# A two-layer diffusion block on one core: GpSimd's weight split and decay masks move to VectorE and TensorE, and column spreads move to ScalarE four at a time

## The chip, the cores and the metric

One core of a Trainium2 chip runs the whole program in one launch. The metric is the device time in microseconds; the kernel before was timed three times. A profile of one further execution gives the rows below. Engines in them: PE is TensorE (PEld its weight loads), DVE is VectorE, ACT is ScalarE, POOL is GpSimd, SP is SyncE, which here issues most DMAs.

## The reference, cut to what matters

Two layers follow each other over 256 latent and 256 context tokens of width 1024. Layer 0 mixes with latent attention plus retention, layer 1 (the second mixer) with a gated delta net; after each mixer comes a layer of 16384 experts (`peer`), which is most of the arithmetic. The change lies mostly in the second mixer:

```python
qkv = jax.nn.silu(short_conv(jnp.concatenate([q, k, v], -1), conv_w))   # z = h @ w_in
q = l2_norm(q) * DN_DK ** -0.5 ; k = l2_norm(k)
decay = jnp.where(incl, jnp.exp(jnp.where(incl, gdiff, 0.0)), 0.0)
lmat = jnp.where(strict, einsum(kb, kc) * decay, 0.0)
t_inv = triangular_solve(eye + lmat, eye)
attn = einsum(qc, kc) * decay
y = rms_norm(o, norm_g) * silu(gate)          # gated_out
```

## The kernel before, in words

All of it is one program of Python loops; the framework's scheduler orders each engine's queue, and each queue then runs strictly in that order, an instruction waiting at its head for what it needs. Full precision is had from three fp32r products: `split` (L262) makes a high part (ACT copies to fp32r, L268) and a low part (a subtraction, L271), and `mm3` (L256) multiplies high by high, high by low and low by high.

The second mixer is `deltanet`. Its stages in the trace:

- 1729 to 2057 us, projections and inverses. `heads` takes 32 weight chunks of 128x1024 (`weights`, L1234: DMA `dw`, ACT `dwsh`, GpSimd `dwsl`, two buffers each), multiplies (`dz`), convolves over five taps (ACT the first, DVE four: L1320, L1322, tile `cv`), and normalises q and k: squares, column sums, `rstd_steps` on DVE (tiles `r4..`, `r2..`, `dr`), then `row_bcast` per 128 tokens. At the same time `inv_rows` builds the triangular matrices `BT` from `decay` (tile `E`) and key products, `inv_solve` (L1415, L1416) solves their 32-blocks on DVE one step after another, and `inv_join` joins the blocks.
- 2057 to 2146 us, the recurrence over chunks (`recur`), with `queries`, which calls `decay` again for q (`Eq`).
- 2146 to 2196 us, `gated`: the root-mean-square of each head's output, its spread (`orb`), the gate, the output product `yo`.

`row_bcast` (L357) turns a column of 128 values into a row that stands in all partitions: DVE multiplies a tile of ones by the column (tile `gcol`, 128x128, three buffers), and PE multiplies it by the identity. Four calls fill one 512-wide PSUM tile. It is called 16 times in `gated`, 48 times in `heads`, 8 times in `low` (first mixer) and 48 times in `gate_row`. `decay` (L1363) makes on PE the sums of the log decays, exponentiates on ACT, and GpSimd multiplies by a 0/1 mask (L1372), 16 times for the inverses and 8 times for the queries.

Of the kernel before, what the change touches and what calls it, by code (L numbers as in the profile page):

```python
# [10 lines left out]
F32 = mybir.dt.float32  # L11
F32R = mybir.dt.float32r
# [4 lines left out]
ALU = mybir.AluOpType  # L17
# [4 lines left out]
P = 128  # L22
D = 1024
KD = D // P
# [218 lines left out]
class Model:  # L243
# [102 lines left out]
    def gate_row(self, pool, ps, l, m, s):  # L346
        nc = self.nc
        t = pool.tile([P, D], F32, name=f"gate{l}{m}{s}")
        for h in range(2):
            o = ps.tile([P, 512], F32, tag="ps", name=f"adag{l}{m}{s}{h}")  # L350
            for k in range(4):
                self.row_bcast(pool, o[:, k * P:(k + 1) * P], self.mod[l, m][:, h * 4 + k, s:s + 1])
            nc.scalar.copy(t[:, h * 512:(h + 1) * 512], o)
        return t


    def row_bcast(self, pool, out, col):  # L357
        self.n += 1
        g = pool.tile([P, P], F32, tag="gcol", name=f"gcol{self.n}", bufs=3)
        self.nc.vector.tensor_scalar_mul(g, self.c["ones"], col)  # L360
        self.mm(out, g, self.c["ident"])

    def rstd(self, out, x, scale, eps):

# [98 lines left out]
    def mixer0(self, open_x, open_h):  # L463
        nc, a, c = self.nc, self.a, self.c
# [15 lines left out]
        rg = pq.tile([P, 4, T2], F32, name="rg")  # L480
# [17 lines left out]
        with ExitStack() as e2:  # L498
            p = self.pool(e2, "m0ada", 1, side="right")
# [13 lines left out]
        p1 = self.pool(ep, "m0t", 1, side="right")  # L513
# [15 lines left out]
        def low():  # L529
            sqs = []  # L530
            for j in range(3):
                nc.scalar.copy(cq[:, j, :], zs[j])
                sq = p1.tile([P, T2], F32, tag="sq", name=f"sq{j}", bufs=3)
                nc.scalar.activation(sq, cq[:, j, :], AF.Square)
                sqs.append(sq)
            yield

            ss = ps.tile([P, 8], F32, tag="ps", name="cqss")
            for tb in range(4):
                sl = slice(tb * P, (tb + 1) * P)  # L540
                self.mm(ss[:, tb:tb + 1], sqs[0][:, sl], c["ones"][:, :1], True, False)
                self.mm(ss[:, tb:tb + 1], sqs[1][:, sl], c["ones"][:, :1], False, True)
                self.mm(ss[:, 4 + tb:5 + tb], sqs[2][:, sl], c["ones"][:, :1])
            v = p1.tile([P, 8], F32, name="cqv")
            nc.vector.tensor_scalar(v[:, :4], ss[:, :4], 1.0 / 256, 1e-6, ALU.mult, ALU.add)
            nc.vector.tensor_scalar(v[:, 4:], ss[:, 4:], 1.0 / 128, 1e-6, ALU.mult, ALU.add)
            r = p1.tile([P, 8], F32, name="cqr")
            nc.scalar.activation(r, v, AF.Sqrt)
            nc.vector.reciprocal(r, r)
            nc.vector.tensor_mul(v, v, r)  # L550
            nc.vector.tensor_mul(v, v, r)
            nc.vector.tensor_scalar(v, v, -0.5, 1.5, ALU.mult, ALU.add)
            nc.vector.tensor_mul(r, r, v)
            yield
            for b in range(2):
                o = ps.tile([P, T2], F32, tag="ps", name=f"cqb{b}")
                for tb in range(4):
                    self.row_bcast(p1, o[:, tb * P:(tb + 1) * P], r[:, b * 4 + tb:b * 4 + tb + 1])
                for i in ((0, 1), (2,))[b]:
                    g = qn[:, i:i + 1] if i < 2 else kvn  # L560
                    nc.vector.scalar_tensor_tensor(cq[:, i, :], cq[:, i, :], g, o, ALU.mult, ALU.mult)
                    nc.scalar.copy(cs[0][:, i, :], cq[:, i, :])
                    nc.vector.tensor_sub(cs[1][:, i, :], cq[:, i, :], cs[0][:, i, :].bitcast(F32))
            yield
            w = pw.tile([P, 512], F32, tag="w", name="uv", bufs=2)
            nc.sync.dma_start(w, a["uv"])
            ws = self.split(pw, w, [P, 512], "arw")
            yield
            for tb in range(4):
                o = ps.tile([P, 512], F32, tag="ps", name=f"vm{tb}")  # L570
                sl = slice(tb * P, (tb + 1) * P)
                self.mm3(o, (cs[0][:, 2, sl], cs[1][:, 2, sl]), ws, True, True)
                nc.scalar.copy(VM[:, tb, :], o)
# [62 lines left out]
        p = self.pool(ea, "m0at", 3)  # L636
# [133 lines left out]
        with ExitStack() as e2:  # L770
            p = self.pool(e2, "m0o", 1, side="right")
            w = []
            for k in range(KD):
                r = p.tile([P, D], F32, tag="woutr", name=f"woutr{k}", bufs=3)
# [5 lines left out]
            x = open_x()  # L780
            p = self.pool(e2, "m0n", 1, side="right")
# [14 lines left out]
            h = open_h()  # L796
# [416 lines left out]
    def deltanet(self, hs, next_h, open_x, ahead, xt):  # L1213
        nc, a, c = self.nc, self.a, self.c
# [10 lines left out]
        p = self.pool(es, "dn", 1, side=side)  # L1225
# [8 lines left out]
        def weights(src, nm):  # L1234
            w = pw.tile([P, KD, P], F32, tag="w", name="dw" + nm, bufs=2)
            nc.sync.dma_start(w, src)
            return self.split(pws, w, [P, KD, P], "dws", bufs=2, eng=nc.gpsimd)


        def gates(pw, pv):  # L1240
# [45 lines left out]
            nc.vector.tensor_scalar_mul(sm["negc"], sm["negc"], -1.0)  # L1286

        cw, known = c["dn_conv"], set()

        def heads(kind, h0, pool, bufs, ps):
# [58 lines left out]
            for i in range(2):  # L1351
                h = h0 + i
                o = ps.tile([P, 512], F32, tag="ps", name=f"qb{n}{i}")
                for tb in range(nb):
                    self.row_bcast(pv, o[:, tb * P:(tb + 1) * P], r[:, i, tb:tb + 1])
                if kind == 0:
                    nc.vector.scalar_tensor_tensor(qT[:, h, :], cv[:, i, :], P ** -0.5, o[:, :T], ALU.mult, ALU.mult)
                else:
                    nc.vector.tensor_mul(kT[:, h, :], cv[:, i, :], o)
                    known.add(h)  # L1360


        def decay(pool, tg, h0, d, n, tag, bufs):  # L1363
            mr, ml = (("le", "gt"), ("ge", "lt"))[d]
            u = slice(d * 8 + h0, d * 8 + h0 + 4)
            rg = pool.tile([P, 4, P], F32, tag="rg", name="rg" + n, bufs=2)
            nc.vector.tensor_tensor(rg, c[mr].unsqueeze(1).broadcast_to([P, 4, P]), sm["g"][:, tg, u].unsqueeze(2).broadcast_to([P, 4, P]), ALU.mult)
            o = ps.tile([P, 512], F32, tag="ps", name="gd" + n)
            self.mm(o, c[ml], rg.rearrange("p u i -> p (u i)"))
            E = pool.tile([P, 4, P], F32, tag=tag, name="E" + n, bufs=bufs)  # L1370
            nc.scalar.activation(E, o.rearrange("p (u i) -> p u i", u=4), AF.Exp)
            nc.gpsimd.tensor_mul(E, E, c[mr].unsqueeze(1).broadcast_to([P, 4, P]))  # L1372
            return E, rg


# [242 lines left out]
        def gated(h):  # L1618
            ov = oT[:, h:h + 2, :]
            sq = po.tile([P, 4, P], F32, tag="sq", name=f"osq{h}")  # L1620
            nc.scalar.activation(sq, ov.rearrange("p h (b t) -> p (h b) t", t=P), AF.Square)
            o = ps.tile([P, 4], F32, tag="ps", name=f"oss{h}")
            for i in range(4):
                self.mm(o[:, i:i + 1], sq[:, i, :], c["ones"][:, :1])
            r = po.tile([P, 4], F32, tag="r", name=f"or{h}")
            self.rstd(r, o, 1.0 / P, "e6")
            yield
            o = ps.tile([P, 512], F32, tag="ps", name=f"orb{h}")
            for i in range(4):
                self.row_bcast(po, o[:, i * P:(i + 1) * P], r[:, i:i + 1])  # L1630
            nc.vector.scalar_tensor_tensor(ov, ov, ng, o.rearrange("p (h t) -> p h t", h=2), ALU.mult, ALU.mult)
            nc.vector.scalar_tensor_tensor(ov, ov, 0.5, gT[:, h:h + 2, :], ALU.mult, ALU.mult)
            nc.scalar.copy(yh[:, h:h + 2, :], ov)
            nc.vector.tensor_sub(yl[:, h:h + 2, :], ov, yh[:, h:h + 2, :].bitcast(F32))
            yield
            for k in (h, h + 1):
                w = po.tile([P, D], F32, tag="w", name=f"wo{k}", bufs=2)
                nc.sync.dma_start(w, a["dn_out"][:, k, :])
                ws = self.split(po, w, [P, D], "wo", bufs=3)
                for tb in range(NTB):  # L1640
                    for hf in range(2):
                        if k == 0:
                            ys.append(ps.tile([P, 512], F32, tag="ps", name=f"yo{tb}{hf}"))
                        sl, hl = slice(tb * P, (tb + 1) * P), slice(hf * 512, (hf + 1) * 512)
                        self.mm3(ys[tb * 2 + hf], (yh[:, k, sl], yl[:, k, sl]), (ws[0][:, hl], ws[1][:, hl]), k == 0, k == KD - 1)
# [150 lines left out]
```

## Time and profile before

| | us |
|---|---|
| runs | 3101.31, 3096.46, 3106.05 (median 3101.31) |
| the profiled execution's own time | 3091.57 |
| its span, first to last instruction | 3089.8 |
| PE busy | 2792.0 (90%) |
| DVE busy | 2307.7 (75%) |
| ACT busy | 1272.9 (41%) |
| POOL busy | 747.8 (24%) |

Busy shares are over the whole span, most of which is the two expert stages; the change acts in 467 us of it, from 1729 to 2196 us, so the stage's own rows have to be read.

### The profile page before, as it was taken

What the parts mean: (1) busy time and instruction counts of PE and PEld (TensorE: products, weight loads), DVE (VectorE), ACT (ScalarE), POOL (GpSimd) and SP (SyncE); (2) the same over time, 40 slices, a digit from 0 to 9 for tenths busy, and PEclk for the clock granted to TensorE, in tenths of its full rate; (3) what the DMA queues carried; (4) which work ended last, traced back from release to release, by engine and by line L of the source; (5) the groups of instructions that cost most, each with busy time, mean ns of one, the idle gap of its engine ahead of it and who ended that gap; (6) DMA issues with size and microseconds to landing.
All of it is one profiled execution on the core that took longest, in us unless ns stands there. A gap on an engine that the chain in (4) does not pass through costs nothing.

```text
span 3089.8 us, 44817 instructions
## 1 busy us (share of the span) xinstructions
PE 2792.0 (90%) x16843; PEld 2424.3 (78%) x16843; DVE 2307.7 (75%) x4500; ACT 1272.9 (41%) x2141; POOL 747.8 (24%) x469
## 2 busy tenths in 40 slices
PE   8989999988999799999999778668888899999997
PEld 4766788877789688888899566657887789999996
DVE  2966599996999899999544687877799665555555
ACT  3235333683333233333333335322348454444443
POOL 2310234001045756665000234414320100000000
PEclk9989999999999899999999889779899999999999
DMA  6531323669999799999542112322347876666663
GB/s 232 183 117 35 109 83 133 231 253 332 323 374 400 289 399 377 395 399 375 180 150 94 68 54 82 91 56 76 129 147 263 284 241 216 207 213 209 213 211 109
DMA packets 272170, 643.87 MB, mean 208 GB/s; under 512 B 36464, under 2 KB 138992, under 8 KB 267472
## 3 DMA queue, kind: packets, MB, share of 16 engines
q1 hardware_dynamic: 225120, 487.50, 47.0%
q0 software_dynamic: 38768, 142.49, 11.9%
q10 hardware_dynamic: 8064, 11.01, 1.0%
q8 instruction: 132, 2.16, 0.3%
q14 instruction: 86, 0.70, 0.1%
HBM read 583.77 MB, written 57.15 MB: 207 GB/s over the span
## 4 chain that ended last, share of the span: by engine, by line
PE 38%; DVE 16%; DMA 11%; issue 6%; POOL 4%; ACT 3%; POOLq 0%; SPq 0%; ACTq 0%; DVEq 0%
PE f L254 16%; PE act L254 15%; DMA vr<-p_v 3%; DMA rowv<-p_v,rowe 3%; DMA ur<-p_u 2%; DVE cv L1322 2%; PE dz L254 2%; POOL rowv L1061 1%; POOL rowu L1061 1%; DVE vsl L271 1%; DVE usl L271 1%; DVE rowy L1078 1%; DVE adaj L341 1%; DVE rowu L1068 1%; DMA adat<-ada_t 1%
## 5 line engine op out<-in xcount | busy, mean ns | idle before, releaser
L254 PE MATMUL f<-vsl,gsh 128*128 128x512 f32 x1260 | 498.3, 397 | 28.6 <-DVE vsl L271 28.5
L254 PE MATMUL f<-vsh,gsh 128*128 128x512 f32 x1260 | 489.6, 397 | 21.7 <-ACT gsh L268 14.1
L254 PE MATMUL f<-vsh,gsl 128*128 128x512 f32 x1260 | 495.4, 395 | 4.6 <-DVE gsl L271 4.6
L271 DVE TENSOR_TENSOR vsl<-vr,vsh 128x1024 fp32r<-128x1024 f32 x252 | 303.9, 1238 | 192.4 <-ACT vsh L268 191.5
L271 DVE TENSOR_TENSOR usl<-ur,ush 128x1024 fp32r<-128x1024 f32 x240 | 295.0, 1229 | 165.3 <-ACT ush L268 161.5
L268 ACT ACTIVATE ush<-ur 128x1024 fp32r<-128x1024 f32 x256 | 270.0, 1055 | 261.5 <-PE act L254 168.2
L254 PE MATMUL act<-hp0h,usl 128*128 128x384 f32 x1024 | 346.7, 339 | 15.7 <-DVE usl L271 12.9
L254 PE MATMUL act<-hp0h,ush 128*128 128x384 f32 x1024 | 347.9, 340 | 5.2 <-ACT ush L268 4.3
L254 PE MATMUL act<-hp0l,ush 128*128 128x384 f32 x1024 | 345.2, 337 | 0.0
L268 ACT ACTIVATE vsh<-vr 128x1024 fp32r<-128x1024 f32 x252 | 257.2, 1052 | 213.0 <-PE f L254 139.7
L268 ACT ACTIVATE gsh<-gelu 128x384 fp32r<-128x384 f32 (+1 forms) x256 | 119.9, 470 | 498.5 <-DVE gelu L1168 395.8
L254 PEld LDWEIGHTS f<-vsl,gsh 128*128 128x128 f32 x1260 | 240.1, 191 | 84.2 <-DVE vsl L271 38.0
L254 PEld LDWEIGHTS f<-vsh,gsh 128*128 128x128 f32 x1260 | 238.6, 191 | 78.3 <-ACT vsh L268 17.3
L254 PE MATMUL act<-hp1h,usl 128*128 128x256 f32 x1024 | 294.2, 287 | 4.6 <-DVE usl L271 4.6
L254 PE MATMUL act<-hp1h,ush 128*128 128x256 f32 x1024 | 295.0, 288 | 1.2 <-ACT ush L268 1.2
L254 PE MATMUL act<-hp1l,ush 128*128 128x256 f32 x1024 | 294.6, 288 | 0.0
L254 PEld LDWEIGHTS f<-vsh,gsl 128*128 128x128 f32 x1260 | 239.7, 190 | 55.7 <-DVE gsl L271 6.0
L1061 POOL DMA_INDIRECT rowu<-p_ur,rowe x128 | 175.2, 1369 | 279.0 <-DVE rowa L1068 182.7
L1061 POOL DMA_INDIRECT rowv<-p_v,rowe x128 | 186.9, 1460 | 95.5 <-DVE rowy L1078 72.0
L254 PEld LDWEIGHTS act<-hp0h,usl 128*128 128x128 f32 x1024 | 193.8, 189 | 18.7 <-DVE usl L271 14.5
L254 PEld LDWEIGHTS act<-hp1h,usl 128*128 128x128 f32 x1024 | 200.3, 196 | 5.9 <-DVE usl L271 5.6
L254 PEld LDWEIGHTS act<-hp1h,ush 128*128 128x128 f32 x1024 | 200.3, 196 | 3.6 <-ACT ush L268 1.4
(773 smaller groups left out, 5961.1 us busy)
## 6 DMA issues: line engine op xcount, KB each, us to landing
ur<-p_u SPq DMA_DIRECT2D x256, 512.0 KB, 4.5
vr<-p_v SPq DMA_DIRECT2D x256, 512.0 KB, 4.5
adat<-ada_t SPq DMA_DIRECT2D x80, 512.0 KB, 5.8
W<-wst SPq DMA_DIRECT2D x20, 2048.0 KB, 7.3
w<-W SPq DMA_DIRECT2D x32, 768.0 KB, 9.6
wq<-p_wq SPq DMA_DIRECT2D x32, 512.0 KB, 3.4
dw<-dn_in SPq DMA_DIRECT2D x32, 512.0 KB, 3.3
w<-W SPq DMA_DIRECT2D x32, 512.0 KB, 5.6
```

The source lines that it names most:

```text
L254: self.nc.tensor.matmul(out, l, r, start=start, stop=stop)
L268: nc.scalar.activation(hi, x, AF.Copy)
L271: (eng or nc.vector).tensor_sub(lo, x, hi.bitcast(F32))
L341: nc.vector.tensor_tensor_reduce(j, w, self.crow[:, s, :], op0=ALU.mult, op1=ALU.add, scale=1.0, scalar=self.c["ada_c"][:, l, m, k:k + 1], ...
L1061: nc.gpsimd.indirect_dma_start(t, None, tabs[z], bass.IndirectOffsetOnAxis(ap=self.e[:, s:s + 1], axis=0))
L1068: nc.vector.tensor_tensor_reduce(u, u, self.h, op0=ALU.mult, op1=ALU.add, scale=1.0, scalar=0.0, accum_out=self.act[:, s:s + 1])
L1078: nc.vector.scalar_tensor_tensor(self.y, rows.pop((1, v)), self.g[:, v:v + 1], self.y, ALU.mult, ALU.add)
L1322: (nc.gpsimd if CONV[j] == "p" else nc.vector).scalar_tensor_tensor(co, xp[:, :ns, q:q + T], cw[:, j, q:q + 1], co, ALU.mult, ALU.add)
```

## The change

Four edits. (1) `weights` of the second mixer no longer names GpSimd, so the low part `dwsl` is computed by DVE. (2) `decay` loses GpSimd's mask; a second product is added to the same PSUM tile instead, an identity `one` times a mask that is 0 inside and -16384 outside, so that the exponential gives zero outside. (3) `row_bcast` becomes `rows_bcast`: one broadcast copy writes four (or two) columns' tiles at once, 128x512 (or 128x256), and all callers give it to ACT. (4) `gate_row` uses it with a single buffer.

```diff
-    def row_bcast(self, pool, out, col):
+    def rows_bcast(self, pool, out, cols, eng, bufs=2):
+        nc, n = self.nc, cols.shape[1]
         self.n += 1
-        g = pool.tile([P, P], F32, tag="gcol", name=f"gcol{self.n}", bufs=3)
-        self.nc.vector.tensor_scalar_mul(g, self.c["ones"], col)
-        self.mm(out, g, self.c["ident"])
+        g = pool.tile([P, 4, P], F32, tag="gcols", name=f"gcols{self.n}", bufs=bufs)[:, :n, :]
+        x = cols.unsqueeze(2).broadcast_to([P, n, P])
+        if eng == "act":
+            nc.scalar.copy(g, x)
+        else:
+            nc.vector.tensor_copy(g, x)
+        for j in range(n):
+            self.mm(out[:, j * P:(j + 1) * P], g[:, j, :], self.c["ident"])
...
-            for k in range(4):
-                self.row_bcast(pool, o[:, k * P:(k + 1) * P], self.mod[l, m][:, h * 4 + k, s:s + 1])
+            self.rows_bcast(pool, o, self.mod[l, m][:, h * 4:h * 4 + 4, s], "act", 1)
...
-            return self.split(pws, w, [P, KD, P], "dws", bufs=2, eng=nc.gpsimd)
+            return self.split(pws, w, [P, KD, P], "dws", bufs=2)
...
+        one = p.tile([P, P], F32R, name="one")
+        nc.scalar.copy(one, c["ident"])
+        out_of = [p.tile([P, P], F32R, name=f"out{d}") for d in range(2)]
+        for t, m in zip(out_of, ("le", "ge")):
+            nc.vector.tensor_scalar(t, c[m], 1.0, 16384.0, ALU.subtract, ALU.mult)
...
-                for tb in range(nb):
-                    self.row_bcast(pv, o[:, tb * P:(tb + 1) * P], r[:, i, tb:tb + 1])
+                self.rows_bcast(pv, o, r[:, i, :], "act")
...
-            self.mm(o, c[ml], rg.rearrange("p u i -> p (u i)"))
+            self.mm(o, c[ml], rg.rearrange("p u i -> p (u i)"), True, False)
+            self.mm(o.rearrange("p (u i) -> p u i", u=4), one, out_of[d].unsqueeze(1).broadcast_to([P, 4, P]), False, True)
             E = pool.tile([P, 4, P], F32, tag=tag, name="E" + n, bufs=bufs)
             nc.scalar.activation(E, o.rearrange("p (u i) -> p u i", u=4), AF.Exp)
-            nc.gpsimd.tensor_mul(E, E, c[mr].unsqueeze(1).broadcast_to([P, 4, P]))
```

The calls in `low` and `gated` change like the one in `heads`.

The scheduler orders the queues anew. On POOL, in the middle of the projections, stood before low parts (`dwsl`) and masks (`E`) by turns:

```order
L271 TENSOR_TENSOR dwsl_15703<-dw_15700,dwsh_15702 128x1024
L271 TENSOR_TENSOR dwsl_15767<-dw_15764,dwsh_15766 128x1024
L1372 TENSOR_TENSOR E_15690<-E_15690,small 128x512
L1372 TENSOR_TENSOR E_15697<-E_15697,small 128x512
L271 TENSOR_TENSOR dwsl_15893<-dw_15890,dwsh_15892 128x1024
L271 TENSOR_TENSOR dwsl_15970<-dw_15967,dwsh_15969 128x1024
```

and now POOL goes from the previous norm straight to the solve's start values (`Tt`) and the spreads of the joins (`XA`):

```order
L447 TENSOR_TENSOR hp0l<-hf_14831,hp0h 128x256
L447 TENSOR_TENSOR hp0l<-hf_14845,hp0h 128x256
L1419 MEMSET Tt_16132 128x1024
L1420 MEMSET Tt_16132 128x32
L1450 TENSOR_TENSOR XA<-r_16444,small 128x512
L1419 MEMSET Tt_16135 128x1024
```

All 32 low parts and 24 masks are gone from POOL; the spreads stay. On DVE, around the small step `negc` (L1286 before, L1290 now), stood before:

```order
L360 TENSOR_SCALAR gcol_15521<-c_ones,dr_15458 128x128
L360 TENSOR_SCALAR gcol_15524<-c_ones,dr_15458 128x128
L360 TENSOR_SCALAR gcol_15527<-c_ones,dr_15458 128x128
L1286 TENSOR_SCALAR negc<-negc 128x64
L1322 SCALAR_TENSOR_TENSOR cv_15322<-xp_15427,small,cv_15322 128x512 x4
```

and now:

```order
L379 TENSOR_SCALAR r4z_15395<-r4a_15393 128x8
L271 TENSOR_TENSOR dwsl_15487<-dw_15484,dwsh_15486 128x1024
L1290 TENSOR_SCALAR negc<-negc 128x64
L1332 SCALAR_TENSOR_TENSOR cv_15268<-xp_15361,small,cv_15268 128x512
L380 TENSOR_SCALAR r4y_15394<-r4z_15395 128x8
L1332 SCALAR_TENSOR_TENSOR cv_15268<-xp_15361,small,cv_15268 128x512
```

The spreads have left DVE's queue, and a weight's low part stands in it ahead of the convolution of the chunk two before it.

## Rows read from the trace of the kernel before

**Rows 1.** Busy time by stretch: stretch and length, then busy us (count) per engine, PE clock, DMA.
```profile
1729.00:2057.00 328.00, 242.32 (x1784) 206.15 (x1784) 259.24 (x595) 121.75 (x237) 123.27 (x69) 0.81 0.26 74
2057.00:2146.00 89.00, 84.96 (x1024) 74.46 (x1024) 60.25 (x144) 24.77 (x57) 22.32 (x17) 0.96 0.13 40
2146.00:2196.00 50.00, 38.90 (x176) 32.12 (x176) 39.71 (x61) 17.82 (x24) 13.03 (x7) 0.80 0.54 184
```
**Rows 2.** Groups by line, 1729 to 2057: count, busy us, mean ns, idle before.
```profile
L271 POOL TENSOR_TENSOR dwsl<-dw,dwsh 128x1024 fp32r<-128x1024 f32 x32 | 79.2, 2477 | 161.7 <-ACT dwsh L268 151.5 <-DVE xp L1317 4.1 <-DMA dw<-dn_in 3.6
...
L1372 POOL TENSOR_TENSOR E<-E,small 128x512 f32<-128x512 f32 x16 | 24.0, 1512 | 19.9 <-ACT E L1371 10.2 <-DVE rg L1367 8.1 <-DVE dg L1402 1.6
...
L1395 DVE SCALAR_TENSOR_TENSOR BT<-kk,beta,E 128x128 f32<-128x128 f32 x64 | 19.6, 339 | 11.1 <-PE kk L254 6.0 <-POOL E L1372 5.0
L360 DVE TENSOR_SCALAR gcol<-c_ones,dr 128x128 f32<-128x128 f32 x48 | 19.1, 424 | 4.1 <-PE qb L254 3.9
```
**Rows 3.** Timeline of POOL and DVE, two pairs from 1761 and 2025.
```profile
1761.56 2.40 POOL L271 TENSOR_TENSOR dwsl<-dw,dwsh 128x1024 fp32r<-128x1024 f32 x1 [3.87 <-ACT dwsh L268]
...
1761.69 2.35 DVE L1272 TENSOR_TENSOR g<-g,spd 128x64 f32<-128x64 f32 x1
...
1764.30 0.23 DVE L1272 TENSOR_TENSOR g<-g,spd 128x64 f32<-128x64 f32 x1
...
2025.11 2.39 POOL L271 TENSOR_TENSOR dwsl<-dw,dwsh 128x1024 fp32r<-128x1024 f32 x1 [13.07 <-ACT dwsh L268]
...
2025.87 2.43 DVE L1322 SCALAR_TENSOR_TENSOR cv<-xp,small,cv 128x256 f32<-128x256 f32 x2 [0.67 <-ACT cv L1320]
```
**Rows 4.** Waits, 1729 to 2057: us in total, times, longest.
```profile
ACT dwsh L268 <- PE dz L254: 46.2, 9, 13.4
ACT dwsh L268 <- issue: 38.3, 6, 15.3
PE qb L254 <- DVE gcol L360: 37.9, 11, 9.7
...
DVE cv L1322 <- ACT cv L1320: 20.2, 5, 16.5
```
**Rows 5.** One tile, `wol`: DVE's own low part of a 128x1024 weight (min/median/max ns).
```profile
L271 DVE TENSOR_TENSOR wol<-wo,woh x8: 1211/1222/1227, 2165.8 to 2189.0; 128x1024 fp32r<-128x1024 f32 x8
```
**Rows 6.** Tile `gcol`, all of the span: min/median/max ns.
```profile
L360 DVE TENSOR_SCALAR gcol<-c_ones,dr x48: 238/280/2410, 1782.0 to 2052.2; 128x128 f32<-128x128 f32 x48
```
**Rows 7.** ACT groups, 1729 to 2200: copies of 512 and 256 columns, the weight's high part.
```profile
L268 ACT ACTIVATE dwsh<-dw 128x1024 fp32r<-128x1024 f32 x32 | 33.8, 1058 | 94.4 <-PE dz L254 46.2 <-issue 38.3 <-DMA dw<-dn_in 5.7
...
L1318 ACT COPY xp<-dz 128x512 f32<-128x512 f32 x16 | 9.1, 570 | 0.0
...
L1318 ACT COPY xp<-dz 128x256 f32<-128x256 f32 x8 | 2.9, 358 | 1.1 <-PE dz L254 1.1
```
**Rows 8.** Chain of waits, an fp32r product stretch of 128x512 at full clock.
```profile
2506.11 5.75 PE act L254 x48
2511.86 5.47 PE f L254 x24
```
**Rows 9.** Groups by line, 2057 to 2146: masks of the queries and their readers.
```profile
L1372 POOL TENSOR_TENSOR Eq<-Eq,small 128x512 f32<-128x512 f32 x8 | 10.6, 1328 | 38.8 <-ACT Eq L1371 38.8
L1534 DVE TENSOR_TENSOR AT<-qk,Eq 128x512 f32<-128x512 f32 x8 | 5.1, 686 | 6.2 <-POOL Eq L1372 3.2 <-PE qk L254 3.1
```
**Rows 10.** Timeline of POOL and DVE, 2152 to 2161 (`gated` and the affine of the previous norm).
```profile
2152.42 3.08 DVE L360 TENSOR_SCALAR gcol<-c_ones,or 128x128 f32<-128x128 f32 x3 [0.25 <-PE orb L254]
...
2153.07 4.66 POOL L420 TENSOR_TENSOR xl<-xl,lg 128x1024 f32<-128x1024 f32 x2 [6.14 <-DVE gcol L360]
...
2156.08 1.74 DVE L360 TENSOR_SCALAR gcol<-c_ones,or 128x128 f32<-128x128 f32 x1
...
2157.70 5.10 POOL L421 TENSOR_TENSOR xl<-xl,lb 128x1024 f32<-128x1024 f32 x2
...
2157.74 2.85 DVE L1632 SCALAR_TENSOR_TENSOR oT<-oT,x 128x512 f32<-128x512 f32 x1
```
**Rows 11.** Timeline of PE, 83 to 98 (first mixer, spread `cqb`).
```profile
86.24 3.44 PE L254 MATMUL cqb<-small,gcol 128*128 128x128 f32 x12 [5.88 <-DVE gcol L360]
...
92.78 0.49 PE L254 MATMUL cqb<-small,gcol 128*128 128x128 f32 x2 [0.42 <-DVE gcol L360]
```
**Rows 12.** Tile `adag` (`gate_row`), all of the span: its waits (us, times).
```profile
  PE adag L254: 9.9, 8
  DVE gcol L360: 3.0, 4
```

More of the change, by code (lines that the diff above doesn't have):

```diff
@@ L556, in low @@
                 o = ps.tile([P, T2], F32, tag="ps", name=f"cqb{b}")
-                for tb in range(4):
-                    self.row_bcast(p1, o[:, tb * P:(tb + 1) * P], r[:, b * 4 + tb:b * 4 + tb + 1])
+                self.rows_bcast(p1, o, r[:, b * 4:b * 4 + 4], "act")
                 for i in ((0, 1), (2,))[b]:
@@ L1628, in gated @@
             o = ps.tile([P, 512], F32, tag="ps", name=f"orb{h}")
-            for i in range(4):
-                self.row_bcast(po, o[:, i * P:(i + 1) * P], r[:, i:i + 1])
+            self.rows_bcast(po, o, r, "act")
             nc.vector.scalar_tensor_tensor(ov, ov, ng, o.rearrange("p (h t) -> p h t", h=2), ALU.mult, ALU.mult)
```

## The prediction, made before the changed kernel was run

> **What bounds the kernel now.** I first looked for the stretch that the change touches, and then, there, for the engine that has least room. By stretch [rows 1], the projections and inverses take 328 us: DVE is busy for 259 of them (79%), PE for 242 at a mean granted clock of 0.81, ACT for 122, POOL for 123. No engine is full, but DVE is the fullest, and it is full because of POOL. The timeline shows how: POOL starts a low part at 1761.56 for 2.40 us; DVE starts a 64-column product at 1761.69 and ends it 2.35 us later, as POOL ends; the same product takes 0.23 us at 1764.30 [rows 3]. So a POOL subtraction of two SBUF tensors holds DVE's next instruction of that kind until it is over. The last low part, at 2025.11, does the same to a convolution tap [rows 3].
>
> I took every DVE instruction of 1729 to 2060, less the lower quartile of its shape: 45 were stretched by over 0.5 us, the second and one of the last stand in the pairs above, and the stretch sums to 70 us. By what POOL ran meanwhile, 50.5 us fall to low parts, 6.3 to masks, 13.4 to the joins' spreads. The same can be seen in a single group: a `gcol` takes 0.28 us in the median and 2.41 at worst [rows 6], which makes its mean 0.424 [rows 2].
>
> The waits come next [rows 4]: PE waited 37.9 us for `gcol` before a spread (`qb`), so normalisation stalls PE; ACT waited 46.2 us for PE before a weight's high part, and 38.3 us more for something that the profile does not name.
>
> From 2057 to 2146 PE is the bound (85 of 89 us), and from 2146 to 2196 a chain over DVE, ACT and PE [rows 1].
>
> **The change part by part.**
>
> *Low parts to DVE.* Removed: 32 POOL subtractions, 79.2 us [rows 2], and with them the 50.5 us of held DVE. Added on DVE: 32 x 1.222 us = 39.1, the duration of the same subtraction where DVE does it already [rows 5]. Net on DVE: -11.4 us. Per piece, 1.58 us of being held against 1.22 us of working: a small margin, and the part of which I am least sure.
>
> The row shows that DVE pays for GpSimd's work, so to take that work over costs DVE little. The Trainium skill, "Perfetto Trace Analysis", section "Optimizing Scalar/DVE Operations", says that with DVE saturated it may make sense to offload work to Scalar or even GpSimd, and warns that GpSimd and DVE share a port. Its first half speaks against this edit and is the fourth rival below; by its warning the sum is as here.
>
> *New waits on DVE.* A low part in DVE's queue waits for ACT's high part (1.058 us [rows 7]), and that for PE to be done with the chunk two before it. Behind it stand convolutions, the solve and the norms. The trace does not have this wait. Its lower end is 0: POOL's queue stood in the same place, and DVE mostly arrives late. Its upper end is POOL's own wait for ACT, 151.5 us [rows 2], which is mostly POOL having nothing else to do. The nearest row is the 20.2 us that DVE waited for ACT before a convolution [rows 4], 16.5 of them once, before the stage had filled. The order puts a low part just ahead of the convolution of a chunk whose product must be ready anyway, so I take a third of one ACT split each: 32 x 1.06 / 3, rounded to +10 us.
>
> *Masks.* 16 POOL products of 1.51 us go from the inverses [rows 2]: -6.3 us of held DVE and -5.0 us that DVE waited for them before `BT`. In their place PE gets 16 products of 128x512. A run of 24 such fp32r products takes 5.47 us [rows 8], 0.23 each, 0.46 at half clock; PE idles 86 us of this stretch, so only the latency in the chain from sums to exponential counts: +1.5 us by estimate. Net -9.8 us.
>
> *Spreads.* 48 `gcol` go from DVE: 48 x 0.28 = 13.4 us (the rest of their 19.1 us is held time that is counted above), and 3.9 us in which DVE waited for a free buffer [rows 2]. ACT gets 8 copies of 512 columns and 8 of 256, by the nearest copies 0.570 and 0.358 us [rows 7]: 7.4 us on an engine busy 37% of the stretch; its cover is that idle time, and if it is gone, at most those 7.4 us come back. Net -17.3 us.
>
> Sum for DVE: -11.4 - 9.8 - 17.3 = -38.5 us. Not all of it is on the path. I take DVE's busy share of the stretch, 0.79: -30.4. With the new waits: **-20.4 us**.
>
> *Recurrence.* Eight masks go, for which DVE waited 3.2 us [rows 9]; eight PE products come, 8 x 0.23 = 1.8 us on the engine that is the bound. Zero, give or take 2.
>
> *`gated`.* Three spreads take 3.08 us and a fourth 1.74 on DVE instead of 0.28 each, since GpSimd's affine of the previous norm runs beneath them; the gate product after them is held until 2160.59 [rows 10]. One ACT copy of 0.57 us does not stand behind POOL, so the first gate product comes between two POOL instructions and not after the fourth: up to -5 us. ACT has one copy more before each of four heads. I take -4.
>
> *Elsewhere.* In the first mixer PE waited 5.88 us before the spread, of which most is DVE's norm and stays; a copy saves the interrupted fourth columns, 0.42 [rows 11]: -0.5. The twelve gate rows: the waits on them sum to 13 us over the span [rows 12], and a row's second copy now waits for PE to release its single buffer; zero, give or take 3.
>
> Sum: -20.4 - 4 - 0.5 = **-24.9 us**. From the profiled execution's own 3091.57 that is 3066.7. The median of the runs is 9.7 us above that execution, so against it the forecast is 3101.31 - 24.9 = **3076 us**.
>
> **The rivals.**
>
> *More than that (0.14).* PE's 37.9 us before the spreads lie on the path beside DVE's load, as PE's low clock and the longest single wait of 9.7 us suggest. Against it: those waits are DVE being held, counted once already. With half of them on top, -25 - 19 = -44: 3057 us.
>
> *No gain (0.14).* The stretch is paced by the ring of two weight buffers, PE product to ACT's high part to low part to PE product, and DVE's saving turns into idle time. For it: ACT's 46.2 and 38.3 us before the high part. Against it: PE and DVE were busy while ACT waited. Only the 4 us of `gated` and about 1 us remain: 3096 us.
>
> *Slower, by waiting in line (0.06).* Place: DVE's queue at each `dwsl`. Mechanism: a low part not yet ready holds the solve and convolutions that are, which POOL's own queue never did. Price: the mean wait times 32. It decides from (30.4 + 4.5) / 32 = 1.1 us each; at 1.8 us, about one ACT split and two thirds, it is 58 - 35 = +23: 3124 us. For it: ACT waited 84.5 us before 32 high parts, 2.6 us each. Against it: in the new order other DVE work of the same chunk is due at the same point.
>
> *Slower, by load (0.02).* DVE counts at face value: +39.1 for low parts, -13.4 - 3.9 for spreads, nothing for held time, +22 x 0.79 = +17, less 2 for `gated`: 3116 us. The stretched instructions speak against it plainly.
>
> That the low parts stay on POOL is out: none is in its new queue.
>
> **How the numbers follow.** The forecast, -12 to -38 us, has 0.64. I call 0.3% (9.3 us) what a measurement of this kernel can tell from no change. Faster: 0.64 + 0.14 + 0.02 of the no-gain case = 0.80. Within 0.3%: the other 0.12. Slower: 0.06 + 0.02 = 0.08. The range runs from the larger case, 3054, to just past the no-gain case, 3098: the new waits between 0 and 34 us (32 whole ACT splits) give 3066 to 3100 by themselves, and all of DVE's 38.5 on the path without waits gives 3058.
>
> **What would show each step.** Right: no DVE instruction of 64 columns above 1 us between the first `dwsl` and the joins; DVE's busy time in the projections down by about 30 us; `dwsl` on DVE at 1.2 us; PE's wait before `qb` under 15 us; the stretch of 328 us at about 308; `gated` at about 46. Wrong: DVE idle before `dwsl` above 35 us in total, the stretch unchanged with DVE's busy time down (the ring), or PE's waits moved from `gcol` to ACT's copies. A time below 3050 or above 3100 would make the prediction wrong.

## The result, and the profile after

| | before | changed |
|---|---|---|
| median of the runs shown together, us | 3099.08 (3096.46 to 3106.05, 4 runs) | 3057.43 (3055.93 to 3068.62, 4 runs) |
| ratio, 95% interval | | 0.9861 [0.9833, 0.9889] |
| the profiled execution's own time, its span | 3091.57, 3089.8 | 3056.68, 3054.9 |

The change made the kernel 41.7 us faster; the forecast was 24.9 us faster (3076 us), and the range 3054 to 3098 holds the result. The direction was right and the gain was undersized: it lies beyond the forecast's own band of 12 to 38 us.

By stretch, the changed kernel (columns as in [rows 1]; projections and inverses, recurrence, `gated`):

```profile
1732.00:2014.00 282.00, 228.92 (x1764) 195.96 (x1763) 218.94 (x580) 129.15 (x255) 20.23 (x22) 0.88 0.28 81
2014.00:2102.00 88.00, 85.08 (x1076) 75.21 (x1076) 58.63 (x148) 25.61 (x59) 12.14 (x10) 0.99 0.14 46
2102.00:2152.00 50.00, 35.76 (x176) 29.79 (x174) 34.20 (x39) 20.77 (x30) 15.72 (x7) 0.83 0.55 187
```

Against [rows 1], the first stretch went from 328 to 282 us. DVE's busy time in it went from 259.24 to 218.94, so 40.3 us less; what is left of the stretch, DVE's idle time, went from 69 to 63 us. The saving on DVE arrived whole: the stretch lost 46 us. PE's granted clock rose from 0.81 to 0.88 and its busy time fell by 13 us.

The groups by line of that stretch answer to [rows 2] and [rows 7]:

```profile
L271 DVE TENSOR_TENSOR dwsl<-dw,dwsh 128x1024 fp32r<-128x1024 f32 x32 | 39.0, 1222 | 19.9 <-ACT dwsh L268 18.8 <-POOL hp0l L447 1.2
...
L1404 DVE SCALAR_TENSOR_TENSOR BT<-kk,beta,E 128x128 f32<-128x128 f32 x64 | 19.2, 346 | 0.4 <-ACT E L1381 0.3
...
L254 PE MATMUL qb<-small,gcols 128*128 128x128 f32 x96 | 18.7, 361 | 30.9 <-ACT gcols L362 30.7
...
L254 PE MATMUL gd<-out,one 128*128 128x512 f32 x16 | 12.4, 776 | 0.0
...
L362 ACT COPY gcols<-dr 128x512 f32<-128x512 f32 x8 | 4.7, 615 | 0.1
```

The low part costs DVE 1.222 us, exactly the price taken from `wol` [rows 5]. The wait of `BT` for the mask is gone (11.1 us to 0.4). The new wait of `dwsl` for ACT's high part is there, 18.8 us in 8 waits.

And its waits, beside [rows 4]:

```profile
ACT dwsh L268 <- PE dz L254: 63.1, 19, 9.0
...
PE qb L254 <- ACT gcols L362: 30.7, 8, 8.0
DVE dwsl L271 <- ACT dwsh L268: 18.8, 8, 6.5
```

ACT's 38.3 us before `dwsh` that the profile did not name are gone; its wait for PE grew from 46.2 to 63.1. PE still waits 30.7 us before the spreads, now for ACT.

In `gated`, the timeline of POOL and DVE answers to [rows 10]:

```profile
2108.04 0.75 DVE L1639 SCALAR_TENSOR_TENSOR oT<-oT,small,orb 128x512 f32<-128x512 f32 x1 [1.54 <-PE orb L254]
...
2108.82 0.69 DVE L1640 SCALAR_TENSOR_TENSOR oT<-oT,x 128x512 f32<-128x512 f32 x1
...
2110.09 2.34 POOL L425 TENSOR_TENSOR xl<-xl,lg 128x1024 f32<-128x1024 f32 x1 [6.68 <-DMA lg<-ln_g]
...
2110.49 3.03 DVE L271 TENSOR_TENSOR usl<-wq,ush 128x1024 fp32r<-128x1024 f32 x1
```

The gate product that was held for 2.85 us now takes 0.69, as forecast. But GpSimd's affine, which now starts after that product, holds what follows in DVE's queue: `usl` (3.03 us in place of 1.22), a `yl` (2.83 in place of 0.68) and the next gate product (2.73 in place of 0.69). Behind these stands the first `wol`, the low part for which the output product then waits 5.3 us:

```profile
2116.74 2.83 DVE L1642 TENSOR_TENSOR yl<-oT,yh 128x512 fp32r<-128x512 f32 x1
...
2119.59 2.73 DVE L1640 SCALAR_TENSOR_TENSOR oT<-oT,x 128x512 f32<-128x512 f32 x1
```

```profile
PE yo L254 <- DVE wol L271: 5.3, 1, 5.3
```

### The profile page after: what moved, and what is told of

It is laid out like the page before. It is cut to its first block, busy times and chain, and to the rows that moved or that the text cites. A ratio compares the mean times of both kernels' runs of the same rounds, so it can differ in the third digit from the quotient of the medians.

```text
span 3054.9 us, 44722 instructions
## 1 busy us (share of the span) xinstructions
PE 2773.7 (91%) x16867; PEld 2412.5 (79%) x16867; DVE 2249.5 (74%) x4414; ACT 1291.4 (42%) x2176; POOL 643.4 (21%) x413
## 4 chain that ended last, share of the span: by engine, by line
PE 35%; DVE 13%; issue 9%; DMA 8%; POOL 5%; ACT 3%; POOLq 0%; DVEq 0%; ACTq 0%; SPq 0%
PE f L254 14%; PE act L254 13%; DMA rowv<-p_v,rowe 3%; PE dz L254 3%; DMA vr<-p_v 2%; POOL rowv L1065 2%; POOL rowu L1065 2%; DMA ur<-p_u 1%; DVE usl L271 1%; DVE vsl L271 1%; DVE cv L1332 1%; DVE rowu L1072 1%; PE qb L254 1%; DVE adaj L341 1%; DVE rowy L1082 1%
```

## The experiments

All kernels are in one table: the one before, the changed one (run twice) and eleven others. Each ratio is to the kernel before, run beside it. The stretch runs from the first product of the projections to the first product of the recurrence, rounded to whole us, with DVE's busy time in it, and what is left, its idle time.

| kernel | median us (runs) | ratio to before | stretch | DVE busy | DVE idle |
|---|---|---|---|---|---|
| before | 3099 to 3102 | 1 | 321 | 257.4 | 63.6 |
| masks alone | 3090.37 (12) | 0.9966 [0.995, 0.9982] | 310 | 252.3 | 57.7 |
| spreads alone | 3085.55 (9) | 0.9957 [0.9939, 0.9974] | 306 | 241.5 | 64.5 |
| split alone | 3076.01 (6) | 0.9903 [0.9877, 0.9929] | 289 | 235.0 | 54.0 |
| changed, split undone | 3076.05 (4) | 0.9929 [0.991, 0.9948] | 299 | 235.3 | 63.7 |
| changed | 3057.43 (4) | 0.9861 [0.9833, 0.9889] | 278 | 216.6 | 61.4 |
| changed, again | 3062.47 (4) | 0.9859 [0.9831, 0.9887] | 284 | 216.5 | 67.5 |
| changed, GpSimd load back | 3108.63 (10) | 1.0024 [1.0005, 1.0043] | 328 | 279.0 | 49.0 |
| changed, GpSimd copy added | 3073.44 (4) | 0.9913 [0.9897, 0.993] | 291 | 236.5 | 54.5 |
| changed, DVE work added | 3079.48 (4) | 0.9914 [0.9886, 0.9941] | 297 | 245.1 | 51.9 |
| changed, spreads on DVE | 3066.7 (4) | 0.9888 [0.9855, 0.9921] | 284 | 217.4 | 66.6 |
| changed, gate rows as before | 3048.45 (5) | 0.9833 [0.9809, 0.9856] | 278 | 216.6 | 61.4 |
| changed, first mixer's split too | 3040.91 (4) | 0.9814 [0.9787, 0.9841] | 279 | 216.6 | 62.4 |
| changed, both of these | 3047.13 (5) | 0.98 [0.9774, 0.9826] | 285 | 217.0 | 68.0 |

Two readings come before the single runs. First, the changed kernel, twice profiled, shows a stretch of 278 and 284 us with the same DVE busy time, so a difference of 6 us in the stretch is not an effect. Outside the stretch single profiles differ more: the first product of the second mixer comes between 1727 and 1752 us, and already at 1733, 1731 and 1752 us in three kernels that do the same work ahead of it (before, masks alone, split alone). Second, DVE's busy time runs from 217 to 279 us and the stretch follows it, while the idle time stays between 49 and 68. One thing limits what a single edit shows: the scheduler orders the queues of every kernel anew.

### The three edits, one by one

Split alone: the kernel before with

```diff
-            return self.split(pws, w, [P, KD, P], "dws", bufs=2, eng=nc.gpsimd)
+            return self.split(pws, w, [P, KD, P], "dws", bufs=2)
```

> The kernel before with the low parts on DVE and nothing else. Theory H (GpSimd's two-input instructions hold DVE, and what DVE gets back passes whole to the end): DVE gives 39 us of work for 50 us of being held, so 10 to 18 us faster; DVE's stretched instructions in the projections fall from 70 us to about 20. Theory P (the gain came from TensorE no longer waiting for spreads, and DVE's load counts at its face value): 10 to 20 us slower.

Measured 3076.01, ratio 0.9903: some 25 us faster, as much as the forecast's whole sum and more than either theory gave this edit. The stretch lost 32 us.

```profile
1752.00:2041.00 289.00, 230.76 (x1777) 197.27 (x1778) 235.02 (x622) 120.46 (x235) 42.79 (x36) 0.87 0.27 78
```

DVE took over 39.0 us of work and is still 22.4 us less busy. By the mean durations of the same instructions in the two kernels, 52.4 us of stretching went, 13.4 net. Most of the 9 us between the two measures is overlap: busy time counts records that overlap once, and DVE's overlap by 36.6 us here and by 29.7 in the kernel before. Counted as in the prediction, 20 us of stretching are left of the 70, as theory H had it.

Masks alone: the kernel before with the change's edit (2), the added product for the mask (and the two constants that it multiplies):

```diff
-            self.mm(o, c[ml], rg.rearrange("p u i -> p (u i)"))
+            self.mm(o, c[ml], rg.rearrange("p u i -> p (u i)"), True, False)
+            self.mm(o.rearrange("p (u i) -> p u i", u=4), one, out_of[d].unsqueeze(1).broadcast_to([P, 4, P]), False, True)
...
-            nc.gpsimd.tensor_mul(E, E, c[mr].unsqueeze(1).broadcast_to([P, 4, P]))
```

> The kernel before with the mask product in place of GpSimd's mask and nothing else. Theory H: 6 us of being held and 5 us of waiting go, 8 to 12 us faster. Theory P: the products lengthen TensorE's queue by 5 us and nothing is won, within 5 us of before.

3090.37 us, ratio 0.9966 and a stretch 11 us shorter, as the first theory had it.

Spreads alone: the kernel before with the change's edits (3) and (4), so `rows_bcast` for all callers, on ACT; in the second mixer:

```diff
-                for tb in range(nb):
-                    self.row_bcast(pv, o[:, tb * P:(tb + 1) * P], r[:, i, tb:tb + 1])
+                self.rows_bcast(pv, o, r[:, i, :], "act")
```

> The kernel before with the four-column spreads by ScalarE, everywhere, and nothing else. Theory H: 13 us of DVE's work and 4 us of its waits go, 14 to 20 us faster. Theory P: TensorE's 38 us of waits before the spreads are the gain, 30 us or more faster, nearly all of what the whole change brings.

3085.55 us, ratio 0.9957, a stretch 15 us shorter, near the first theory's 14 to 20. The theory by which the load decides (split slower, spreads 30 us faster) is refuted by the first and the third run.

In the stretch the three parts bring 32 + 11 + 15 = 58 us alone and 37 to 43 together. In DVE's busy time they nearly add: 22.4 + 5.1 + 15.9 = 43.4 against 40.8. So what doesn't add is idle time, which split alone had also lowered by 10 us and which comes back when all is done.

The changed kernel with the split undone (the first of these diffs, reversed):

> The changed kernel with the second mixer's low parts back on GpSimd: masks by an added product and spreads on ACT stay. If the parts simply add, the split is worth what is left of the stretch's 42 us when masks (10) and spreads (15) alone are taken off: 17 us, stretch near 296, time near 3074. If the split alone was worth 32 us because it frees VectorE from being held, and masks and spreads then overlap with it, it is worth 25 to 32 here too: stretch 303 to 311, time 3082 to 3090. VectorE's stretched instructions about 50 us in both.

3076.05 us and a stretch of 299: the split is worth 14 to 19 us as the last of the three, against 25 as the first; in the stretch 15 to 21, against 32. The parts simply add in this direction; the second expectation (25 to 32) did not hold. The stretched instructions sum to 59 us, a little above the 50 that both expected.

### Is it the holding?

In the changed kernel, GpSimd gets a subtraction per weight that nobody waits for:

```diff
-            return self.split(pws, w, [P, KD, P], "dws", bufs=2)
+            hi, lo = self.split(pws, w, [P, KD, P], "dws", bufs=2)
+            scr = pws.tile([P, KD, P], F16, tag="scr", name="scr" + nm, bufs=1)
+            nc.gpsimd.tensor_sub(scr, w, hi.bitcast(F32))
+            return hi, lo
```

> The changed kernel, and per weight of the second mixer one more GpSimd subtraction of two SBUF tensors (128x1024, about 2.4 us) into a scratch tile that nothing reads: the low part of the product still comes from VectorE. Theory H (VectorE's held instructions were the price of the split on GpSimd, and their saving passes whole to the stretch): VectorE's stretched instructions sum to 35 to 55 us again in the projections (8.0 in the changed kernel), the stretch goes from 278 to 308-330 us, the time is 3085 to 3110. Rival C (what the split on VectorE brought is that a low part is ready 1.2 us sooner and in an emptier queue, on the chain weight, high part, low part, product): a result that nobody waits for costs nothing there, stretch 275 to 288 us, time 3050 to 3067.

3108.63 us: the whole gain is gone, and a little more. DVE's instructions beneath these subtractions were stretched by 56.7 us, just above theory H's 35 to 55, and the stretch grew by 44 to 50. Apart from the added subtraction the queue is nearly the same: of the 575 DVE instructions in the changed kernel's stretch, 573 stand in the same order here. Windows, and two of DVE's neighbours in the timeline:

```profile
1727.00:2055.00 328.00, 239.19 (x1793) 204.13 (x1794) 279.03 (x577) 127.46 (x252) 110.07 (x53) 0.83 0.25 69
```

```profile
1764.89 2.45 POOL L1243 TENSOR_TENSOR scr<-dw,dwsh 128x1024 f16<-128x1024 f32 x1 [5.68 <-DMA dw<-dn_in]
...
1765.02 2.37 DVE L1280 TENSOR_SCALAR g<-g 128x64 f32<-128x64 f32 x1
...
1768.24 0.19 DVE L1280 TENSOR_SCALAR g<-g 128x64 f32<-128x64 f32 x1
```

A DVE instruction of 0.19 us takes 2.37 because GpSimd computes something useless. By itself this run does not refute rival C, the earlier low part on the weight's chain. The subtraction holds the low part too (13.1 of the 56.7 us), so from the end of a high part to the end of its low part 5.1 us pass in the mean, 2.6 in the changed kernel, and PE waits for it:

```profile
PE dz L254 <- DVE dwsl L271: 16.8, 6, 8.2
```

Two other kernels speak against the rival as the main cause. In split alone the low part comes no sooner in the mean than in the kernel before (3.4 us after the high part against 3.0; in the median 1.9 against 2.5), and yet the stretch is 32 us shorter. And with the same addition on DVE (below) the low part is as late as here, at 5.0 us, and the stretch grows by only 13 to 19. A side effect of the subtraction, that a weight's buffer comes free later, is there in both kernels as well: ACT waits 9.0 us for weights still arriving here and 8.8 there, 1.2 in the changed kernel. How much of the 44 to 50 us comes through the late low part is not shown.

With a copy of one tensor in place of the subtraction (`nc.gpsimd.tensor_copy(scr, hi.bitcast(F32))`):

> As the kernel with the unused subtraction, but the unused GpSimd instruction is a copy of one tensor (the high part, 128x1024, to 16 bits). Theory H-two (only GpSimd instructions that read two SBUF tensors hold VectorE): stretched instructions below 15 us, stretch 276 to 288 us, time within 8 us of the changed kernel's. Theory H-any (any GpSimd instruction holds it for as long as it runs): stretched instructions as GpSimd's busy time, 30 us or more, time 3080 or more. If rival C holds, the time is that of the changed kernel too, and the stretched instructions tell which.

3073.44 us, a stretch of 291, 19.6 us of stretching beneath the copies. Neither set of numbers fits, but the timeline decides: one-tensor copies hold DVE as well, only for less long.

```profile
1817.40 1.04 POOL L1243 CAST scr<-dwsh 128x1024 f16<-128x1024 f32 x1 [10.95 <-ACT dwsh L268]
...
1817.42 1.57 DVE L1335 SCALAR_TENSOR_TENSOR cv<-xp,small,cv 128x512 f32<-128x512 f32 x1
...
1825.04 1.23 DVE L271 TENSOR_TENSOR dwsl<-dw,dwsh 128x1024 fp32r<-128x1024 f32 x1 [3.06 <-ACT dwsh L268]
...
1825.14 2.03 POOL L1243 CAST scr<-dwsh 128x1024 f16<-128x1024 f32 x1 [6.69 <-ACT dwsh L268]
```

In the first pair the copy starts first, and the tap takes 1.57 us in place of 0.75. In the second DVE starts first, and the copy takes 2.03 us in place of 1.04. The Trainium skill, "SBUF — State Buffer", section "Who interferes with whom", says that a VectorE instruction with two SBUF inputs contends with a GpSimd instruction that reads SBUF, that it is an exclusive lock, and that the order of issue decides who blocks; both pairs agree with it.

### What DVE's own work costs

The same addition on DVE (`nc.vector.tensor_sub(scr, w, hi.bitcast(F32))`) adds work and no holding:

> The changed kernel, and per weight of the second mixer one more VectorE subtraction of 128x1024 into a 16-bit scratch tile that nothing reads (about 1.2 us, 39 us in all). It prices VectorE's work by itself, with nothing held by GpSimd. If VectorE's work passes to the path by its busy share of the stretch (0.78 after the change): stretch +30 us, 308, time 3088. If it passes whole: +39, 317, time 3097. If a third or more of it falls into VectorE's 63 us of idle time, as the pair of kernels with the split on GpSimd and with an unused GpSimd subtraction suggests (47.6 us of work and holding for 28.6 us of stretch, 0.60): +20 to +26, stretch 298 to 304, time 3077 to 3084.

```profile
L1243 DVE TENSOR_TENSOR scr<-dw,dwsh 128x1024 f16<-128x1024 f32 x32 | 38.9, 1215 | 0.0
```

```profile
PE dz L254 <- DVE dwsl L271: 10.7, 6, 5.3
```

38.9 us of work made the stretch 13 to 19 us longer and the time 17 to 22 us. The time fits the lowest expectation, and the stretch, 297, is just below its 298 to 304. By duration the work costs 16 / 38.9 = 0.41, where held time cost 47 / 56.7 = 0.83 (both from the middle of the two profiles of the changed kernel). Part of that gap is the measure. DVE's records overlap their neighbours, so its busy time grew by only 28.5 us for the 38.9 of work, and by 62.4 for the 56.7 of holding. Per microsecond of busy time the prices are 16 / 28.5 = 0.56 and 47 / 62.4 = 0.75, and the 6 us between the two profiles make them 0.46 to 0.67 and 0.71 to 0.80. The rest of the work falls into idle time, which goes from 61 to 68 us down to 51.9. Why held time falls less into idle time is not shown. That the scheduler orders the queues by the work that it knows of, and knows nothing of the holding, would fit: with the work on DVE only 409 of the 575 DVE instructions keep the changed kernel's order, with the holding 573 do.

### Where the spreads are made

The changed kernel with the spreads of the second mixer's norms by one DVE copy for four (or two) columns, in place of ACT's:

```diff
-                self.rows_bcast(pv, o, r[:, i, :], "act")
+                self.rows_bcast(pv, o, r[:, i, :], "dve")
```

> The changed kernel with the spreads of the second mixer's norms still made four (or two) at once, but by a VectorE copy in place of ACT's. 8 copies of 128x512 and 8 of 128x256 go back to VectorE, by an estimate from its other 512-wide instructions 0.6 and 0.35 us each, 7.6 us in all, and ACT loses its 7.6 us. If the spreads' gain came from VectorE's relief: stretch 3 to 8 us longer, time 3060 to 3066. If it came from joining four small instructions to one, or if the 30.7 us that TensorE waits for ACT's copies cost more than VectorE's work: stretch equal or up to 8 us shorter, time 3049 to 3058.

3066.7 us, but with runs from 3058.25 to 3077.84 and an interval that overlaps the changed kernel's: no difference that these runs can tell. DVE's busy time is 217.4, the same as with the spreads on ACT, though its copies take 6.0 us; its queue is ordered anew, and where the 6 us went is not shown.

```profile
L254 PE MATMUL qb<-small,gcols 128*128 128x128 f32 x96 | 20.5, 394 | 29.3 <-DVE gcols L364 29.3
...
L364 DVE COPY gcols<-dr 128x512 f32<-128x512 f32 x8 | 3.1, 418 | 0.0
```

16 copies of 0.4 us replace 48 instructions that took 19.1 us in the kernel before [rows 2]. So joining them is enough, and between the two engines these runs show no difference. PE's wait before the spread is 29.3 us here and 30.7 with ACT: it is not the choice of the engine that makes PE wait.

### Two further steps

The gate rows as before, one column at a time on DVE, the rest as changed:

```diff
-            self.rows_bcast(pool, o, self.mod[l, m][:, h * 4:h * 4 + 4, s], "act", 1)
+            for k in range(4):
+                self.row_bcast(pool, o[:, k * P:(k + 1) * P], self.mod[l, m][:, h * 4 + k, s:s + 1])
```

> The changed kernel with the gate rows alone spread as before (DVE, one column at a time). If the 6 us that the second expert stage lost between the write-back of its weights and its steady part come from the gate rows' new place in the queues, that part is back at 116 us and the whole is 5 to 8 us faster than the changed kernel. If they are chance or come from elsewhere, the whole is within 3 us of the changed kernel.

3048.45 us, ratio 0.9833 [0.9809, 0.9856]: 9 us below the changed kernel's 3057.43, but the intervals overlap. The stretch is unchanged at 278 us. The second expert stage, from its first `act` product to its last, takes 791.5 us here and 798 to 800 in the two profiles of the changed kernel. Over all profiles it takes 792 to 802 us with the new gate rows (nine) and 792 to 796 with the old (five), so the ranges overlap here too.

The first mixer's low parts on DVE too:

```diff
-            return self.split(pw, w, shape, "arw", eng=nc.gpsimd)
+            return self.split(pw, w, shape, "arw")
```

> The changed kernel, and the first mixer's 20 low parts (2.7 us each on GpSimd) on VectorE as well. In the first 200 us VectorE's instructions are stretched by 31.1 us, all beneath these low parts; 20 x 1.22 = 24.4 us of work come in their place, net 7 us less, and 80 to 160 us is a stretch in which VectorE is busy for 78.7 of 80 us. Theory H: 3 to 10 us faster, 3047 to 3054. Rival: the low parts stand in VectorE's queue behind weights that ACT waits for (44 us for arriving weights), and hold what is queued behind them: 5 to 20 us slower, 3062 to 3077.

Both together:

> The changed kernel with two edits that were the faster side so far: the first mixer's low parts on VectorE (3041 alone) and the gate rows as before, on VectorE one by one (3048 alone). If both are real and independent, 16 and 9 us add: 3028 to 3038, and a ratio of 0.977 to 0.980. If the gate rows' gain was only the spread between runs: 3036 to 3046.

And the changed kernel beside it:

> The changed kernel once more, on the chip and beside the runs that it is compared with: 3055 to 3069, ratio 0.985 to 0.989.

The changed kernel, again, came out as expected: 3062.47 us, 0.9859.

The first mixer's split is the better find: 3040.91 us, 0.9814, more than theory H's 3 to 10 us. In the first 200 us of the changed kernel DVE's instructions are stretched by 31.1 us, all beneath GpSimd's low parts; with the edit by nothing, and the last `rvp<-arwh,h0h` product comes at 177.4 us in place of 186.3. These 9 us are what the trace shows of the gain there. The mean of DVE's group `adaj` in these 200 us shows it (the changed kernel, then this one):

```profile
L341 DVE CUSTOM_DVE_ANT_0 adaj<-adat,c_row,small 128x1024 f16<-128x1024 f32 x48 | 79.1, 1648 | 13.5 <-ACT c_row L330 12.3 <-DMA adat<-ada_t 0.6
```

```profile
L341 DVE CUSTOM_DVE_ANT_0 adaj<-adat,c_row,small 128x1024 f16<-128x1024 f32 x48 | 61.4, 1280 | 4.8 <-ACT c_row L330 3.5 <-DMA adat<-ada_t 1.0
```

Another 6 to 8 us lie in the second expert stage (792.2 us in place of 798 to 800), where the edit changes nothing and profiles differ by as much. The rival, DVE blocked behind weights still on their way, has its wait (35.5 us before `arwl`), but it did not decide. The kernel with both edits has 0.98 [0.9774, 0.9826], clear of the changed kernel's 0.9859 [0.9831, 0.9887] on the same chip: 15 us faster than the change. Its 3047.13 us lie above both expectations in time (3028 to 3038, 3036 to 3046), and its ratio at the upper end of the first. That the gate rows add to the first mixer's split is not shown: with them 0.98, without 0.9814, two intervals that overlap, and the gate rows alone overlap the changed kernel's. Whether the four-at-once gate rows cost a few us stays open.

## Why the prediction was right, and where its sum was not

- **What binds the stretch.** That DVE is full because of POOL was right, and shown by putting a useless subtraction back: DVE's queue is nearly the same, and the gain is gone.
- **The forecast's size.** The 12 to 38 us that it gave 0.64 were missed: 41.7 us faster. The range holds the time only because it reaches down to the larger rival. The stretch came to 282 us where 308 were named.
- **DVE's balance.** Forecast -38.5 us, and DVE's busy time fell by 40.3; that the two are so close is luck. The forecast's sum holds 7.4 us of waits, and its busy time alone was -11.4 - 6.3 - 13.4 = -31.1 ("about 30" among its signs). The three terms were -11.4, -9.8 and -17.3; alone, their kernels show -22.4, -5.1 and -15.9 of busy time, and 32, 11 and 15 us of stretch. Masks and spreads were right in the stretch; the low parts were too small, also as the last of the three (15 to 21 us). Part of it is the price of DVE's own work: 39.1 us was the sum of its records, and records overlap.
- **"Not all of it is on the path. I take DVE's busy share of the stretch, 0.79."** This term failed. The saving passed whole: DVE's idle time was 69 us before and 63 after. A share of busy time is no rate of exchange. Held time and DVE's own work need a price each: by duration 0.83 and 0.41, from the two kernels with a load added. With them the low parts alone come afterwards to -50.5 x 0.83 + 39.1 x 0.41 = -26 us; the split alone measured 32 in the stretch and 25 in time. My net of -11.4 had set the two against each other at par.
- **"With the new waits" +10.** Also mis-sized. The wait exists, 18.8 us before `dwsl`, above the 10 assumed, and costs nothing that can be seen: other waits of DVE went, that for `cv` from ACT from 20.2 to 3.7 us, that of `BT` from 11.1 to 0.4. That the new wait replaced those that stood behind it fits, but was not tested.
- **`gated`.** Forecast -4, measured -0.9 from the last product of the recurrence to the last output product, and a stage of 50 us in place of the 46 named. The mechanism holds up to the first output product, which comes 4.1 us sooner (12.7 us after the recurrence in place of 16.8). The affine then holds `usl`, `yl` and the next gate product instead, and PE waits 5.3 us for `wol`; at the first product with `wol` 1.5 us of the gain are left.
- **Recurrence.** Forecast 0, measured -4.3. From its first product to its last it takes 91.5 us before and 87.2 now. Masks alone also show it (87.8). Of the eleven profiles without the eight masks of the queries ten take 87 to 90 us, the three with them 91 to 92, so it belongs to these masks; with DVE work added it takes 93.4, which is not explained. The mask products cost more by their records than the 0.23 to 0.46 us assumed (0.776 in the projections), but records of PE overlap, and its busy time in the recurrence stayed: 84.96 us before, 85.08 now.
- **PE's wait before `qb`.** Forecast under 15 us, measured 30.7. I took it for the effect of held DVE instructions; it stayed when these were gone, and also with the copy on DVE (29.3). This is one of the prediction's own signs of being wrong: PE's waits moved from `gcol` to ACT's copies. So what it said of these waits failed; what makes them is open.
- **Elsewhere.** Forecast -0.5. Between the two profiles the three stages of the second mixer gained 47 us and the span 34.9, so some 12 us went elsewhere: 2.9 before the second mixer's first product and 8.1 in the second expert stage. Profiles differ by as much at the same work, so this is not laid to the change.
- **The rivals.** The result lies at the time of "more than that" (3057), but not by its mechanism: PE's waits for the spreads, which that rival took off the path, are still there. "No gain", by the ring of weight buffers, is out: ACT's wait for PE before `dwsh` grew to 63.1 us, and DVE's idle time did not grow. "Waiting in line" needed 1.1 us a piece and got 18.8 / 32 = 0.6. "Load" is refuted by split alone.

What stays open: why the parts do not add in the stretch, what of the gain is PE's higher clock (0.81 to 0.88 came along with the change and was never changed by itself), and what of a single edit's effect is the queues' new order.

## What to carry to other kernels

Look for short VectorE instructions that take ten times their usual duration, and at what GpSimd runs meanwhile: here work on GpSimd that reads SBUF was paid for by VectorE. It was cheaper to give VectorE 39 us of work than to let GpSimd hold it for 50. Don't multiply a saving on the fullest engine by its busy share; price held time and added work apart, each by a kernel that adds only that, and see that the rest of the queue keeps its order.

## What the runs showed of the hardware

That a GpSimd copy of one tensor holds VectorE, I had not expected: 19.6 us in all for 32 copies. The holding also goes both ways: GpSimd's subtraction takes 2.34 us at best and 3.40 at worst, the copy 1.04 and 2.09. A GpSimd record that starts inside a VectorE instruction is longer by about what that one has left, as the second pair of the copies shows (0.99 us longer, 1.13 left). Of all 32 each (min/median/max ns):

```profile
L1243 POOL TENSOR_TENSOR scr<-dw,dwsh x32: 2342/2706/3402, 1727.3 to 2024.3; 128x1024 f16<-128x1024 f32 x32
```

```profile
L1243 POOL CAST scr<-dwsh x32: 1036/1404/2091, 1748.2 to 2010.2; 128x1024 f16<-128x1024 f32 x32
```
